# A transformer block on one core: the operands of the MLP's two products as two scaled fp16 pieces instead of two fp32r pieces

## The chip, the core and the metric

The kernel runs on one core of one Trainium2 chip. The core has five engines: TensorE (PE in the profile, with its weight loads as PEld), VectorE (DVE), ScalarE (ACT), GpSimd (POOL) and SyncE (SP), which issues most DMA transfers here. Each engine takes its instructions in order. The metric is the time of one execution on the device in microseconds (us), the median of several.

## What is computed

One block of a transformer for 1024 tokens of width 1024, with float32 in and out:

```python
n = rms_norm(h, norm1_g[layer])
proj = jnp.einsum('bsd,dp->bsp', n, w_in[layer])
...
y = jnp.concatenate([rms_norm(ya, out_norm_a_g[layer]),
                     rms_norm(yb, out_norm_b_g[layer])], axis=-1)
h = h + jnp.einsum('bsm,md->bsd', y, w_out[layer])
n2 = rms_norm(h, norm2_g[layer])
u = jnp.square(jax.nn.relu(jnp.einsum('bsd,df->bsf', n2, w_ff1[layer])))
h = h + jnp.einsum('bsf,fd->bsd', u, w_ff2[layer])
...
return rms_norm(h, final_norm_g)
```

`ya` and `yb` are two groups of attention heads (a sliding window with learned sinks, and chunks with a relative bias). The change is in the last three lines before the final norm: the norm `n2`, the product with `w_ff1` (1024x4096), the squared ReLU, and the product with `w_ff2` (4096x1024).

## The kernel before

The input projection, the attention and the output projection come first (to about 427 us); the change leaves them alone, but its first instructions stand among the last of the output projection. There, for each block `tb` of 128 tokens, PE makes `op_B` (group B's part), and `rows2(tb)` does the rest: DVE multiplies the sum by `rB` (the norm of group B, a short chain of 128x8 operations from `ss_B`) and adds the residual row `h`, ACT takes the sum of squares, `rstd` makes the factor `r` (`u_n2` on ACT, four small operations on DVE), ACT copies the row for its way to DRAM (`hB`), and DVE writes the normed row `n2`. PE transposes pairs of such rows into banks `tp` (two of them), ACT copies them to the tiles `F00` to `F21`, and `operand` splits them, and sums of them, into the operands `X`.

Each product of the MLP is blocked, and each block of two by two parts is multiplied with seven products instead of eight (the numbers 1 to 7; `second_operands` forms the sums and differences of the parts of the weights, `T` for w1 and `Z` for w2). Product 1 goes over eight blocks `n` of 512 hidden columns (`order1`), product 2 over four groups `g` of two such blocks (`order2`). Every one of the 7 x 8 products in each half is 24 matmuls of 128x128 by 128x512: float32 is written as the sum of two pieces, and three of the four products of pieces are taken:

```python
        matmul(ps, a[0], b[0], start=start, stop=False, skip_group_check=shared)
        matmul(ps, a[0], b[1], start=False, stop=False, skip_group_check=shared)
        matmul(ps, a[1], b[0], start=False, stop=stop, skip_group_check=shared)
```

`split` makes the pieces: the high one by a copy on ACT (which rounds), the low one by a subtraction on POOL or DVE. Their type is fp32r before. Operands are named `X` (input of product 1), `W` (its weights, from `T` or a tile `w1`), `U` (the hidden values, read back from DRAM as `u`) and `V` (the weights of product 2, from `Z` or a tile `w2`). The epilogue of product 1 (in `product1`) adds on DVE, takes ReLU and square on ACT, forms the sums for the seven products of the next step in tiles `k` and `v`, and stores them to DRAM (`put`). In product 2, `add_up` adds each finished bank to an accumulator `C` on DVE; `final` makes the last norm.

Operands are prepared two or three products ahead (`AHEAD1`, `AHEAD2`), the loads of `u` three (`LOAD2`). The program's text gives the tile scheduler the order; it may move instructions within what the dependences and the buffers allow, so the order on each engine is shown below where it matters. A buffer pool with a count (`bufs`) makes its next user wait until the oldest tile is free: three pairs of PSUM banks `ab`, two banks `tp`.

## Time and profile before

| | us |
|---|---|
| median of 3 runs (1049.77 to 1051.04) | 1049.78 |
| the profiled execution | 1049.81 |
| its span | 1048.0 |
| first matmul of product 1 / of product 2 | 427.2 / 736.5 |

The profile shows one execution. A row of a group gives source line, engine, operation, output <- inputs, shapes, the count, then the time busy in total and the mean duration in ns. A row of the timeline begins with the start and the duration in us. What an engine waited for is given in brackets or, in the view of waits, as the total, the number and the longest wait.

### The profile page before, as it was taken

How to read it: one execution, taken by the hardware profiler on the slowest of the kernel's cores; microseconds unless marked ns; L12 is line 12 of the kernel's file. 1: busy time of each engine (PE TensorE's matmuls, PEld its weight loads, DVE VectorE, ACT ScalarE, POOL GpSimd, SP SyncE). 2: the span in 40 equal slices, each digit the busy share in tenths (PEclk: the TensorE clock that was granted, in tenths of full speed). 3: DMA queues.
4: the chain of work that ended last, by engine and by line, in shares of the span. 5: the costliest groups of instructions: out<-in, count | busy, mean ns of one | idle time of the engine just before them, and what ended most of it. 6: DMA issues, size and time to landing. Idle time of an engine off the chain costs nothing.

```text
span 1048.0 us, 13827 instructions
## 1 busy us (share of the span) xinstructions
PE 1022.3 (98%) x4803; PEld 829.6 (79%) x4803; DVE 711.9 (68%) x1063; ACT 581.5 (55%) x969; POOL 426.0 (41%) x327
## 2 busy tenths in 40 slices
PE   9999999999988999999999999999999999999997
PEld 7888887777655778878888888887888888888886
DVE  6576787877676635885644554566878777687667
ACT  8676766767567757574454454455523333333346
POOL 0466665243353555015445444545114023124025
PEclk9999999999999999999999999999999999999999
DMA  9944537999999982325524533436996445533004
GB/s 356 252 133 124 141 75 180 199 220 214 225 242 231 221 269 93 119 81 181 181 101 161 181 130 133 178 117 220 375 397 254 147 136 179 170 133 101 1 1 161
DMA packets 141574, 183.77 MB, mean 175 GB/s; under 512 B 78016, under 2 KB 95424, under 8 KB 141504
## 3 DMA queue, kind: packets, MB, share of 16 engines
q1 hardware_dynamic: 141360, 182.63, 58.3%
q8 instruction: 38, 0.62, 0.2%
q14 instruction: 32, 0.26, 0.1%
q10 hardware_dynamic: 144, 0.26, 0.1%
HBM read 103.17 MB, written 42.99 MB: 139 GB/s over the span
## 4 chain that ended last, share of the span: by engine, by line
PE 58%; issue 4%; DVE 1%; ACT 1%; DMA 1%; POOL 0%; ACTq 0%; DVEq 0%; POOLq 0%
PE f L167 24%; PE f_a L167 16%; PE f_c L167 8%; PE op_B L167 4%; PE f_b L167 4%; DMA G_B<-H_B 1%; POOL W L173 0%; PE tp L170 0%; DVE V L173 0%; DVE Z L1245 0%; DVE T L1245 0%; PE end L167 0%; PE op_A L167 0%; DVE k L1316 0%; PE ss_B L167 0%
## 5 line engine op out<-in xcount | busy, mean ns | idle before, releaser
L167 PE MATMUL f<-X,W 128*128 128x512 f32 x1344 | 306.4, 390 | 1.8 <-POOL W L173 1.1
L167 PEld LDWEIGHTS f<-X,W 128*128 128x128 f32 x1344 | 251.9, 188 | 55.1 <-POOL W L173 1.5
L167 PE MATMUL f_a<-V,U 128*128 128x512 f32 x756 | 173.5, 389 | 0.0
L173 POOL TENSOR_TENSOR U<-u,U 128x1024 fp32r<-128x1024 f32 x32 | 80.1, 2502 | 224.9 <-PE f_c L167 135.0
L167 PEld LDWEIGHTS f_a<-V,U 128*128 128x128 f32 x756 | 141.9, 188 | 29.7 <-DVE C L1560 0.3
L173 POOL TENSOR_TENSOR W<-T,W 128x1024 fp32r<-128x1024 f32 x29 | 76.4, 2636 | 103.3 <-ACT W L1267 91.2
L167 PE MATMUL f_c<-V,U 128*128 128x512 f32 x384 | 88.4, 389 | 0.0
L173 POOL TENSOR_TENSOR W<-w,W 128x1024 fp32r<-128x1024 f32 x23 | 59.5, 2587 | 68.8 <-ACT W L1267 62.9
L1267 ACT ACTIVATE V<-Z 128x1024 fp32r<-128x1024 f32 x32 | 33.9, 1060 | 90.3 <-PE f_a L167 44.6
L167 PEld LDWEIGHTS f_c<-V,U 128*128 128x128 f32 x384 | 72.1, 188 | 15.0
L1316 DVE TENSOR_TENSOR k<-f,k 128x1024 f32<-128x1024 f32 x24 | 29.4, 1223 | 79.7 <-PE f L167 42.5
L1267 ACT ACTIVATE W<-T 128x1024 fp32r<-128x1024 f32 x32 | 33.9, 1059 | 66.2 <-PE f L167 26.4
L1267 ACT ACTIVATE V<-w 128x1024 fp32r<-128x1024 f32 x24 | 25.5, 1061 | 81.2 <-issue 34.2
L173 DVE TENSOR_TENSOR V<-w,V 128x1024 fp32r<-128x1024 f32 x24 | 48.9, 2039 | 28.0 <-ACT V L1267 24.6
L167 PE MATMUL op_A<-w_o,y 128*128 128x512 f32 x192 | 57.6, 427 | 8.6 <-DVE ts_vB L427 4.7
L1267 ACT ACTIVATE U<-u 128x1024 fp32r<-128x1024 f32 x56 | 58.5, 1044 | 7.2 <-DMA u<-ud 7.2
L614 ACT ACTIVATE P_B<-P_B,nm_B 128x640 f32<-128x640 f32 (+2 forms) x64 | 44.2, 690 | 29.9 <-DVE nm_B L611 15.0
L859 DVE SCALAR_TENSOR_TENSOR H_B<-P_B,rc_B,H_B 128x640 f16<-128x640 f32 (+2 forms) x64 | 51.7, 836 | 10.4 <-ACT H_B L854 10.0
L167 PE MATMUL ip_qB<-nT,w_qB 128*128 128x512 f32 x192 | 53.8, 406 | 1.1 <-DVE t_kB L401 1.0
L167 PE MATMUL ip_kB<-nT,w_kB 128*128 128x512 f32 x192 | 53.7, 404 | 0.0
L1267 ACT ACTIVATE W<-w 128x1024 fp32r<-128x1024 f32 x24 | 25.3, 1060 | 48.3 <-PE f L167 42.1
L167 PE MATMUL ip_vB<-nT,w_vB 128*128 128x512 f32 x192 | 51.2, 400 | 0.0
(242 smaller groups left out, 1950.2 us busy)
## 6 DMA issues: line engine op xcount, KB each, us to landing
w<-in_w_ff_dram SPq DMA_DIRECT2D x64, 512.0 KB, 4.6
u<-ud SPq DMA_DIRECT2D x56, 512.0 KB, 4.5
ud<-k SPq DMA_DIRECT2D x48, 512.0 KB, 2.9
KkB<-t_kB SPq DMA_DIRECT2D x32, 256.0 KB, 5.1
xr<-in_x_dram SPq DMA_DIRECT2D x8, 512.0 KB, 8.8
st_o<-in_w_out_dram SPq DMA_DIRECT2D x8, 512.0 KB, 5.0
h<-in_x_dram SPq DMA_DIRECT2D x8, 512.0 KB, 4.7
hB<-h SPq DMA_DIRECT2D x8, 512.0 KB, 2.6
```

The source lines that it names most:

```text
L167: pe(nc.tensor.matmul(*args, **kw))
L173: return engine.tensor_tensor(lo, full, f(hi), ALU.subtract)
L614: nc.scalar.activation(pr, pr, AF.Exp, bias=nm, scale=-1.0, accum_out=sm)
L859: nc.vector.scalar_tensor_tensor(lo, q, rc, hi, ALU.mult, ALU.subtract)
L1267: nc.scalar.activation(w[0], full, AF.Copy)
L1316: dve.tensor_tensor(v, ps, v, ALU.add)
```

## The change

All pieces become fp16, and both pieces of an operand lie in one tile. To keep them in fp16's range, each operand is first multiplied by a power of two that is made from the maximum of the data: of g2b, the gain of the norm, for the input (`scale_of_x`, into `xup`, which goes into the norm's factor), of each block of w1 (`see1`, `scale1`: four tiles reduced on DVE, then scaled in place on ACT), of u in each group (maxima taken in the epilogue of product 1, `scale_of_u`), and of w2 in each group (`see2`, `scale2`: eight tiles reduced, the factor `up2` goes into the split). A maximum over all partitions is made by `send`: a column of 128x1 goes to DRAM by SP's queue and is read back to all partitions (128x128, the tile `all`), and `bits` reduces that row on DVE (`topall`). The inverse factors leave with the ReLU (`down1`) and with the sums of product 2 (`down2`). The split on DVE with a factor is a scalar_tensor_tensor; where POOL splits U, ACT scales the tile in place first. The loads of w1 and w2 come earlier: all of `load1(1)` at row block 4, and w2 for a whole group ahead of it, one tile for each product.

```diff
--- before.py
+++ after.py
@@
+PAD = 88
+X_UP, W_UP, U_UP = 7, 12, 11
@@
-    small.tile([P, 8], F32, tag="pad", bufs=1, name="pad")
+    small.tile([P, PAD], F32, tag="pad", bufs=1, name="pad")
@@
+    def bits_of(top, name, least=-90):
+
+        nc.vector.tensor_scalar(top, top, 2.0**least, None, ALU.max)
+        e = small.tile([P, 1], F32, tag="e", bufs=2, name=f"e_{name}")
+        nc.vector.tensor_scalar(e.bitcast(I32), top.bitcast(I32), 0xFF << 23, None, ALU.bitwise_and)
+        return e
+
+    def power(dst, e, by, plus):
+
+        nc.vector.tensor_scalar(dst.bitcast(I32), e.bitcast(I32), float(by), float(plus << 23), ALU.mult, ALU.add)
+        return dst
...
+    class Top:
...
+        def see(self, src):
+            nc.vector.tensor_reduce(self.column(), flat(src), mybir.AxisListType.X, ALU.max, apply_absolute_value=True)
+
+        def send(self):
...
+            nc.vector.tensor_reduce(top, self.cols[:, : self.n], mybir.AxisListType.X, ALU.max)
+            nc.sync.dma_start(tops[self.slot].rearrange("a p -> p a"), top)
+            self.all = small.tile([P, P], F32, tag="all", bufs=1, name=f"all_{self.name}")
+            nc.sync.dma_start(self.all, tops[self.slot][0].partition_broadcast(P))
+
+        def bits(self, least=-90):
+            top = small.tile([P, 1], F32, tag="topall", bufs=3, name=f"topall_{self.name}")
+            nc.vector.tensor_reduce(top, self.all, mybir.AxisListType.X, ALU.max)
+            return bits_of(top, self.name, least)
@@
         r = rstd(ss, D, 1, f"n2_{tb}")
+        nc.vector.tensor_tensor(r, r, xup, ALU.mult)
@@
-            X[p] = [[page([P, 2, HALF], f"X{p}{hl}{i}") for i in range(2)] for hl in range(2)]
-        hi, lo = (X[p][hl][g][:, :, part(n)] for hl in range(2))
+            X[p] = [page16([P, 2, 2, HALF], f"X{p}{i}") for i in range(2)]
+        hi, lo = (X[p][g][:, hl, :, part(n)] for hl in range(2))
         nc.scalar.activation(hi, src, AF.Copy)
-        split_l(engine, lo, src, hi)
+        engine.tensor_tensor(lo, src, hi, ALU.subtract)
@@
+    def see1(n, blocks=((0, 0), (0, 1), (1, 0), (1, 1))):
...
+        for b in blocks:
+            top1[n].see(w1s[(n, *b)])
+        if top1[n].count == 4:
+            top1[n].send()
+
+    def scale1(n):
+        e = top1.pop(n).bits()
+        up1 = power(scale_tile("up1", str(n), 2), e, -1.0, 254 + W_UP)
+        down1[n] = power(scale_tile("down1", str(n), 3), e, 1.0, -W_UP)
+        nc.vector.tensor_tensor(down1[n], down1[n], xdown, ALU.mult)
+        for b in ((0, 0), (0, 1), (1, 1), (1, 0)):
+            w = w1s[(n, *b)]
+            nc.scalar.activation(w, w, AF.Copy, scale=up1)
@@
-    def split(full, name, engine, alloc):
-        w = [alloc(f"{name}{hl}", hl) for hl in range(2)]
-        nc.scalar.activation(w[0], full, AF.Copy)
-        split_l(engine, w[1], full, w[0])
+    def split(full, name, engine, alloc, up=None):
+        w = alloc(name)
+        w = [w[:, hl] for hl in range(2)]
+        if up is not None and engine is pool:
+            nc.scalar.activation(full, full, AF.Copy, scale=up)
+            up = None
+        nc.scalar.activation(w[0], full, AF.Copy, scale=1.0 if up is None else up)
+        if up is None:
+            engine.tensor_tensor(w[1], full, w[0], ALU.subtract)
+        else:
+            engine.scalar_tensor_tensor(w[1], full, up, w[0], ALU.mult, ALU.subtract)
         return w
@@
         if p == 4:
-            nc.scalar.activation(v, ps, AF.Relu)
+            nc.scalar.activation(v, ps, AF.Relu, scale=down1[n])
+            dve.tensor_reduce(top, ps, mybir.AxisListType.X, ALU.max)
         else:
-            dve.tensor_tensor(v, ps, v, ALU.add)
-            nc.scalar.activation(v, v, AF.Relu)
+            dve.tensor_tensor_reduce(v, ps, v, 1.0, 0.0, ALU.add, ALU.max, top)
+            nc.scalar.activation(v, v, AF.Relu, scale=down1[n])
@@
+    scale_of_x()
     rows2(0)
     rows2(1)
     load1(0)
@@
         rows2(tb)
+        if tb in (2, 3):
+            see1(0, ((tb - 2, 0), (tb - 2, 1)))
+        if tb == 4:
+            scale1(0)
         if tb in (4, 5):
             prepare1(0, tb - 3, tb - 4)
-        if tb == 5:
-            load1(1, ((0, 0),))
+        if tb == 4:
+            load1(1)
+        if tb in (6, 7):
+            see1(1, ((tb - 6, 0), (tb - 6, 1)))
+    scale1(1)
     prepare1(1, 1, 2)
-    load1(1, ((0, 1), (1, 0), (1, 1)))
@@
+    def see2(g, tiles):
...
+    def scale_of_u(g):
...
+    def scale2(g):
+        e = top2.pop(g).bits(-30)
+        up2[g] = power(scale_tile("up2", str(g), 2), e, -1.0, 254 + W_UP)
+        down2[g] = power(scale_tile("down2", str(g), 2), e, 1.0, -W_UP)
+        nc.vector.tensor_tensor(down2[g], down2[g], udown[g], ALU.mult)
@@
-        ops2[n, p] = split(a, f"U{n}_{p}", pool if p in (1, 2, 3, 4) else dve, high), split(b, f"V{n}_{p}", dve, third)
+        ops2[n, p] = (
+            split(a, f"U{n}_{p}", pool if p in (1, 2, 3, 4) else dve, high, uup[g]), split(b, f"V{n}_{p}", dve, high, up2[g])
+        )
@@
-        if p == 3 and n > 0:
+        if p == (1 if n > 1 else 5) and n:
             load1(n + 1)
@@
+        if 0 < n < NQ - 1:
+            if p == 6:
+                see1(n + 1)
+            if p == 7:
+                scale1(n + 1)
+        if p == 5 and n and n % GQ == 0:
+            scale_of_u(n // GQ - 1)
+        if (n, p) in ((NQ - 2, 4), (NQ - 1, 1)):
+            for tile2 in blocks2(0)[(p == 1) * 4 :][:4]:
+                load2w(*tile2)
         if n == NQ - 1:
+            if p in (5, 6):
+                see2(0, blocks2(0)[(p == 6) * 4 :][:4])
@@
-        return fp.tile(shape, dt, tag="pg3", bufs=10, name=name)
+        return fp.tile(shape, dt, tag="pg3", bufs=13, name=name)
@@
-        nc.vector.tensor_tensor(flat(c), flat(ps), flat(c), ALU.add)
+        nc.vector.scalar_tensor_tensor(flat(c), flat(ps), down2[g], flat(c), ALU.mult, ALU.add)
@@
     for at, (g, p, n) in enumerate(order2[:-GQ]):
         fetch2(at + LOAD2)
+        step = at % (7 * GQ)
+        if g + 1 < NQ // GQ:
+            if step in range(1, 9):
+                load2w(*blocks2(g + 1)[step - 1])
+            if step in range(3, 11):
+                see2(g + 1, blocks2(g + 1)[step - 3 :][:1])
+            if step == 12:
+                scale2(g + 1)
...
+        if (g, step) == (0, 4):
+            scale_of_u(NQ // GQ - 1)
         prepare2(at + AHEAD2)
```

Where the instructions stand now is shown at three places.

DVE at the end of the output projection of group B. `w_gB` to `rB` is the chain of group B's norm, `op_B_0` and `op_B_1` are the sums of the first two row blocks (`h0`, `h1` their residual rows), `tops_w1_n<-w1_n_..` the reduction of one tile of w1's block n. Before:

```order
L185 TENSOR_SCALAR w_gB_4323<-ss_B_4313 128x8
L186 RECIPROCAL q_gB_4324<-u_gB_4322 128x8
L190 TENSOR_TENSOR w_gB_4323<-w_gB_4323,q_gB_4324 128x8
L191 TENSOR_TENSOR w_gB_4323<-w_gB_4323,u_gB_4322 128x8
L192 RECIPROCAL rB_4252<-w_gB_4323 128x8
L1150 SCALAR_TENSOR_TENSOR op_B_0_4275<-op_B_0_4275,rB_4252,h0_3587 128x1024
L1150 SCALAR_TENSOR_TENSOR op_B_1_4294<-op_B_1_4294,rB_4252,h1_3704 128x1024
```

After (the reductions of the four tiles of w1_0 and that of g2b stand right ahead of this piece):

```order
L1163 TENSOR_REDUCE top_w1_0_4539<-tops_w1_0_4452 128x1
L1140 TENSOR_SCALAR xup__4291<-e_x_4364 128x1
L1140 TENSOR_SCALAR xdown__4292<-e_x_4364 128x1
L1158 TENSOR_REDUCE tops_w1_1_4730<-w1_1_00_4603 128x1
L187 TENSOR_SCALAR w_gB_4341<-ss_B_4331 128x8
L188 RECIPROCAL q_gB_4342<-u_gB_4340 128x8
L192 TENSOR_TENSOR w_gB_4341<-w_gB_4341,q_gB_4342 128x8
L193 TENSOR_TENSOR w_gB_4341<-w_gB_4341,u_gB_4340 128x8
L194 RECIPROCAL rB_4268<-w_gB_4341 128x8
L1207 SCALAR_TENSOR_TENSOR op_B_0_4293<-op_B_0_4293,rB_4268,h0_3603 128x1024
L1170 TENSOR_REDUCE topall_w1_0_4586<-all_w1_0_4542 128x1
L1207 SCALAR_TENSOR_TENSOR op_B_1_4312<-op_B_1_4312,rB_4268,h1_3720 128x1024
```

Ahead of the chain there are now four reductions of 128x1024 for w1_0, one for w1_1 and those for g2b, and the row that needs w1_0's maximum back from DRAM (`topall_w1_0`) stands between the sums of row blocks 0 and 1.

ACT a little later, from the square of row block 0 on (`u_n2_..` is the root in the norm's factor of a row block, `F00` the copy of the first transposed bank). Before:

```order
L1152 ACTIVATE h0_3587,ss2_0_4344<-op_B_0_4275 128x1024
L182 ACTIVATE u_n2_0_4347<-ss2_0_4344,eps4_78 128x1
L1154 ACTIVATE h0_3587<-op_B_0_4275 128x1024
L1152 ACTIVATE h1_3704,ss2_1_4360<-op_B_1_4294 128x1024
L182 ACTIVATE u_n2_1_4363<-ss2_1_4360,eps4_78 128x1
L1154 ACTIVATE h1_3704<-op_B_1_4294 128x1024
L1196 ACTIVATE F00_4431<-tp_00_00_4432 128x2x256
```

After:

```order
L1209 ACTIVATE h0_3603,ss2_0_4369<-op_B_0_4293 128x1024
L184 ACTIVATE u_n2_0_4372<-ss2_0_4369,eps4_78 128x1
L1212 ACTIVATE h0_3603<-op_B_0_4293 128x1024
L1209 ACTIVATE h1_3720,ss2_1_4386<-op_B_1_4312 128x1024
L1315 ACTIVATE w1_0_00_4402<-w1_0_00_4402,up1_0_4591 128x1024
L1315 ACTIVATE w1_0_01_4404<-w1_0_01_4404,up1_0_4591 128x1024
L1315 ACTIVATE w1_0_11_4408<-w1_0_11_4408,up1_0_4591 128x1024
L1315 ACTIVATE w1_0_10_4406<-w1_0_10_4406,up1_0_4591 128x1024
L184 ACTIVATE u_n2_1_4389<-ss2_1_4386,eps4_78 128x1
L1212 ACTIVATE h1_3720<-op_B_1_4312 128x1024
```

Four scalings of w1_0 stand between the square of row block 1 and its root; `u_n2_1` comes four rows of 128x1024 later. The same four for w1_1 stand further on between `h6`'s square and `u_n2_6`, ahead of `h7`'s square and `F20`, the first bank of the last four row blocks.

DVE near the end of group 0 of product 2 (`C` are accumulators, `f2_0_a` PE's banks, `Z` and `V` weights of the next group, `up2_1` their factor). Before:

```order
L1482 TENSOR_TENSOR C110_6876<-f2_0_a_0_6834,C110_6876 128x1024
L1245 TENSOR_TENSOR Z3_6_7483<-w2_3_11_7443,Z3_5_7405 128x1024
L1245 TENSOR_TENSOR Z2_7_7591<-w2_2_11_7403,w2_2_01_7325 128x1024
L1482 TENSOR_TENSOR C111_6878<-f2_0_a_1_6835,C111_6878 128x1024
L173 TENSOR_TENSOR V0_41_7218<-Z0_4_7211,V0_40_7217 128x1024
L1245 TENSOR_TENSOR Z3_7_7629<-w2_3_11_7443,w2_3_01_7363 128x1024
L173 TENSOR_TENSOR V1_41_7258<-Z1_4_7251,V1_40_7257 128x1024
L1482 TENSOR_TENSOR C000_6830<-f2_0_b_0_7221,C000_6830 128x1024
L1482 TENSOR_TENSOR C001_6832<-f2_0_b_1_7222,C001_6832 128x1024
L173 TENSOR_TENSOR V2_11_7296<-w2_2_00_7249,V2_10_7295 128x1024
```

After:

```order
L1158 TENSOR_REDUCE tops_w2_2_7760<-w2_5_00_7834 128x1
L1624 SCALAR_TENSOR_TENSOR C111_7142<-f2_0_a_1_7101,down2_0_6988,C111_7142 128x1024
L1158 TENSOR_REDUCE tops_w2_2_7760<-w2_5_01_7872 128x1
L1170 TENSOR_REDUCE topall_w2_1_7568<-all_w2_1_7492 128x1
L1133 TENSOR_SCALAR topall_w2_1_7568<-topall_w2_1_7568 128x1
L1135 TENSOR_SCALAR e_w2_1_7571<-topall_w2_1_7568 128x1
L1140 TENSOR_SCALAR up2_1_7573<-e_w2_1_7571 128x1
L1140 TENSOR_SCALAR down2_1_7575<-e_w2_1_7571 128x1
L1528 TENSOR_TENSOR down2_1_7575<-down2_1_7575,udown_1_6044 128x1
L1322 TENSOR_TENSOR Z2_5_7646<-w2_2_01_7172,w2_2_00_7130 128x1024
L1158 TENSOR_REDUCE tops_w2_2_7760<-w2_5_11_7909 128x1
L1352 SCALAR_TENSOR_TENSOR V2_1_7582<-w2_2_00_7130,up2_1_7573,V2_1_7582 128x1024
```

Before, DVE's rows here are the sums of finished banks, the differences `Z` and the splits. Now reductions for group 2 (`tops_w2_2`) stand among them, and `V2_1`, the weights of group 1's first product, follows the row that needs group 1's maximum from DRAM (`topall_w2_1`) and the five that make its factors.

95 lines of the change are left out of this document (75 added, 20 removed).

## The prediction

> **What bounds the kernel now.** First the page, then what TensorE (PE) waits for from the output projection of group B (376 us) to the end, then the busy time of each engine stage by stage.
>
> ```profile
> span 1048.0 us, 13827 instructions
> PE 1022.3 (98%) x4803; PEld 829.6 (79%) x4803; DVE 711.9 (68%) x1063; ACT 581.5 (55%) x969; POOL 426.0 (41%) x327
> ...
> PE f L167 <- POOL W L173: 1.1, 1, 1.1
> PE f L167 <- DVE k L1316: 0.5, 1, 0.5
> PE op_B L167 <- ACT o L1049: 0.2, 1, 0.2
> ...
> 503.00:541.00 38.00, 38.00 (x170) 31.47 (x169) 19.62 (x12) 18.52 (x18) 18.08 (x8) 1.00 0.43 152
> 693.00:737.00 44.00, 43.46 (x192) 35.68 (x191) 32.10 (x19) 25.43 (x27) 22.68 (x8) 1.00 0.58 204
> 737.00:813.00 76.00, 76.00 (x337) 62.96 (x336) 61.86 (x47) 28.27 (x29) 20.95 (x8) 1.00 0.91 339
> 813.00:889.00 76.00, 76.00 (x337) 62.93 (x336) 57.72 (x43) 28.01 (x28) 19.28 (x8) 1.00 0.47 153
> ```
>
> PE waits 1.8 us in 672 us. A window's columns are PE, weight loads, DVE, ACT, POOL (each busy us and instructions), the granted clock, DMA share and GB/s. So in the MLP a faster matmul moves the end at once, as long as the next engine follows, and that is DVE: 61.86 of 76 us busy in group 0 of product 2, 19.6 of 38 in product 1. ACT and POOL stay below half. The profiled execution took 1049.8 us, 1.8 outside its span, and equals the median; the sum starts there.
>
> **Matmuls.** Both products are these groups, all 512 columns wide and all fp32r before; a tail of 24 half-wide ones (12 full ones in work) is left out.
>
> ```profile
> L167 PE MATMUL f<-X,W 128*128 128x512 f32 x1344 | 306.4, 390 | 1.8 <-POOL W L173 1.1
> L167 PE MATMUL f_a<-V,U 128*128 128x512 f32 x756 | 173.5, 389 | 0.0
> L167 PE MATMUL f_c<-V,U 128*128 128x512 f32 x384 | 88.4, 389 | 0.0
> L167 PE MATMUL f_b<-V,U 128*128 128x512 f32 x192 | 44.2, 389 | 0.0
> ...
> 375.38 0.66 PE L167 MATMUL av_B<-G_B,VvB 128*128 128x384 f16 x5
> L167 PE MATMUL av_B<-G_B,VvB x8: 219/300/390, 374.1 to 375.8; 128*128 128x512 f16 x2, 128*128 128x384 f16 x2, 128*128 128x256 f16 x2, 128*128 128x128 f16 x2
> ```
>
> An instruction counts in a window when it overlaps it, so the 337 of 737 to 813 share 76 us plus one duration of 0.389: 76.39/337 = 226.7 ns from start to start. For fp16 only the attention has rows. The five at 375.38 are 384, 256, 256, 128 and 128 wide; the last lasts 0.219, so the first four, 1024 columns, take 0.66 - 0.22 = 0.44 us, 220 ns for 512 columns with two starts in it. One start costs 2 to 3 ns if the rest is proportional to the columns, which leaves some 217 and, with the rounding of 0.44, 213 to 220; I take 215. 2676 + 12 matmuls times 11.7 ns is **31.4 us** gained, half in each product (18 at 220 ns, 37 at 213).
>
> The Trainium skill (TensorE: Matmul & The Clock Gate, "Wait — 56ns, not 53.3ns?") gives any warm matmul N/2.4 GHz plus 2.5 ns, 215.7 for 512 columns, and names no type that needs more. By it fp32r would run so already and the gain be nothing; the 226.7 ns here speak against that, the 0.44 us agree for fp16. It is the rival "no faster" below.
>
> **Start of the MLP.** In the rows of the order, DVE now reduces tiles of w1 ahead of rB, and ACT scales four tiles between h1's square and u_n2_1. Before, the same place ran so:
>
> ```profile
> 386.37 0.27 ACT L182 ACTIVATE u_gB<-ss_B,eps 128x8 f32<-128x8 f32 x1 [5.17 <-PE ss_B L167]
> 387.38 0.20 DVE L192 RECIPROCAL rB<-w_gB 128x8 f32<-128x8 f32 x1
> 387.88 2.67 DVE L1150 SCALAR_TENSOR_TENSOR op_B<-op_B,rB,h 128x1024 f32<-128x1024 f32 x2 [0.29 <-PE op_B L167]
> 392.60 0.30 ACT L182 ACTIVATE u_n<-ss,eps 128x1 f32<-128x1 f32 x1
> 393.89 1.28 DVE L1160 SCALAR_TENSOR_TENSOR n<-op_B,r_n,g2b 128x1024 f32<-128x1024 f32 x1 [0.29 <-ACT h L1154]
> 395.87 0.60 PE L170 MATMUL tp<-ident,n 128*128 128x128 f32 x4
> ...
> 382.41 0.37 SPq L123 DMA_DIRECT2D w<-in_w_ff_dram  x1
> DMA to landing us min/median/max: 7.3/7.6/10.1
> ...
> L432 DVE TENSOR_REDUCE top_vB<-ts_vB 128x1 f32<-128x1024 f32 x4 | 4.9, 1218 | 0.1
> L445 ACT ACTIVATE hvB<-ts_vB,up_vB 128x1024 f16<-128x1024 f32 x4 | 4.6, 1138 | 0.2 <-DVE up_vB L435 0.2
> hB<-h SPq DMA_DIRECT2D x8, 512.0 KB, 2.6
> ```
>
> The load of w1_1_00 is the one issued at 382.41; with the shortest landing, 7.3, it is there at 389.7. Its reduction (1.22) and that of w1_0_11 just before stand ahead of the rB chain, with five small ones: rB about 392.4 instead of 387.6, op_B_0's sum 392.7 to 394.0. Then topall_w1_0 waits for a column that goes to DRAM and back: two transfers. No transfer that small has a row; two of the lightest (2.6) are 5.2, the other end is nothing, and I take 5, since the size hardly shows in 2.6 us for 512 KB. Sent near 390, back near 395.2; op_B_1's sum ends about 396.8. ACT: square 1.2, four scalings at 1.14 with a pointer for the scale, 4.5, u_n2_1 starts about 402.4. Before, 2.6 us later (392.60 to 395.17) n2_1 was done, so now about 405.1 with xup's product, and PE's transposition starts there, not at 395.87: **9.2 us** (8.3 if the round trip costs nothing; the reductions and scalings alone make it).
>
> Later, the same with w1_1:
>
> ```profile
> 421.62 1.03 ACT L1152 ACTIVATE h<-op_B 128x1024 f32<-128x1024 f32 x1 [3.36 <-DVE op_B L1150]
> 423.87 0.59 ACT L1205 ACTIVATE F<-tp 128x512 f32<-128x512 f32 x1
> 426.37 1.04 PE L170 MATMUL tp<-ident,n 128*128 128x128 f32 x8
> ...
> 330.87 0.98 PE L167 MATMUL op_A<-w_o,y 128*128 128x512 f32 x3 [2.16 <-ACT o L1049]
> 331.00:334.00 3.00, 3.00 (x12) 1.89 (x13) 2.30 (x5) 3.00 (x7) 1.08 (x1) 0.72 0.86 189
> 334.00:336.00 2.00, 2.00 (x10) 1.48 (x9) 2.00 (x2) 1.03 (x2) 1.88 (x2) 0.57 1.09 230
> ```
>
> After op_B_6's square (421.62 to 422.85) ACT has four scalings 4.5, u_n2_6 0.3, the copy 1.0 and h7's square 1.2 ahead of F20: 429.9, done 430.5. PE's second eight transpositions need its bank, and started at 426.37: **4.2 us**, and nothing covers them, since all products come after. Each wait also costs clock: after 2.16 us of idle PE got 0.72 for 3 us and 0.57 for 2, 0.8 + 0.9 = **1.7 us**, twice. The start costs 16.8 in all; the bounds are 8 (no round trip, w1_1's scalings in a gap, one drop) and 22 (round trips as slow as the 10.1 us above).
>
> **Product 1, then.** Per n of 36.1 us DVE gains four reductions, 4.9, one for u's maximum, 1.2, and some ten small ones at 0.15 to 0.2: 27.5 us, and a wait of 5 for the round trip. It fits; ACT goes from 18.5 to 23. I take 0.5, with 4 as the other end.
>
> **Product 2.** Between 693 and 889 DVE was busy 32.10 + 61.86 + 57.72 = 151.7 us. The rows of the order add there the reductions of w2 for groups 0, 1 and 2 (24 x 1.218 = 29.2), some 42 small ones (7), 40 splits and sums that take a scale (0.06 each, 2.4: n's 1.28 against 1.22) and the end of the last n (1.5): 192 us. The 196 us are now 196 x 215/226.7 = 186. **DVE is 6 us short** where PE was the bound. Below that lies the lead in the ready buffers, which may pay it all; above it lie DVE's waits, since it takes its rows in order: topall_w2_1 stands ahead of V2_1, which group 1's first product needs, and waits for a round trip while DMA is 0.91 busy. DVE idled 14 of the 76 us then. I take **10**, with 0 and 25 as ends. Group 2 and 3 have fewer reductions and catch up. ACT gains eight scalings of U per group, 28 to 37 of 72 us, which is no bound. On SP the loads of w2 move a group ahead, one tile for each product, and the two transfers of a maximum stand between them and the loads of u; the second waits for the first to land, 2.6 us by the light row, while u is asked for three products (15 us) ahead: nothing, as long as that lead holds. The end gains a few 128x1 products: 0.4.
>
> Whether a split with a scale costs 1.28 hangs on these:
>
> ```profile
> L1531 DVE SCALAR_TENSOR_TENSOR fo<-C,rf,gains 128x512 f32<-128x512 f32 x4 | 2.9, 741 | 0.0
> L1216 DVE TENSOR_TENSOR S<-S,F 128x512 f32<-128x512 f32 x4 | 2.7, 682 | 0.0
> L859 DVE SCALAR_TENSOR_TENSOR H_B<-P_B,rc_B,H_B 128x512 f16<-128x512 f32 x8 | 7.2, 896 | 0.0
> ```
>
> 0.06 more at 512 columns; H_B, which reads two tiles of SBUF, has 896, some 0.2 more. At the most 0.4 for 1024 columns would make 16 us of the 40: inside the upper end.
> The Trainium skill (Vector Engine (DVE) Microarchitecture Reference, "7. Points that are easy to get wrong") says that a scalar-tensor-tensor with two SBUF sources that are not bf16 runs at half the rate; the 896 ns for H_B are not twice 682, so the trace does not bear it out.
>
> **Sum.** 1049.8 - 31.4 + 16.8 + 0.5 + 10 + 0.4 = 1046.1.
>
> **Rivals.**
> *All hidden*: the tiles of w1 may land early enough for the rows in front of rB to run before 386.67, and DVE's lead pays for the rest: 1049.8 - 31.4 + 0.4 = 1019. For it: DVE idles a third of the span. Against: the rows in front of rB.
> *Only the start*: DVE's lead covers product 2: 1036.
> *Slower, DVE the bound of group 0 and 1*: its waits cannot be filled, 25 us and more: 1061. It turns the sign once product 2's wait is over 31.4 - 17.7 = 14 us, that is if 8 of the 44 us that DVE idled from 693 to 889 stay, beside the 6. For it: 61.86 of 76 with a saturated DMA; against: most of DVE's idle time there was waiting for PE, which ends when DVE is late.
> *Matmuls no faster*: the first fp16 after an fp32r one starts its successor as late as before, and only runs of up to six are shown. Interval 226.7: 1049.8 + 16.8 + 0.9 = 1067.5, product 2 having the old time again.
> *Scaled splits at half the rate*: 40 x 1.2 more, 1094.
>
> **How the numbers follow.** My forecast 1046 (1039 to 1052) has 0.44; all hidden 0.06; only the start 0.20 (1029 to 1039); slower by DVE 0.20 (1052 to 1068); no faster 0.07; half rate 0.03. Range 1029 to 1064: 0.2 is left out (all hidden, no faster, half rate and the upper edge of the slower case). Within 0.2% (1047.7 to 1051.9, about what a measurement here can tell from no change) lies 0.14 of the forecast's 0.44; faster is the rest of it below, 0.28, with 0.26 of two rivals, 0.54; slower the others and its edge, 0.32.
>
> **What would show it.** In the profile after: windows of 76 us in product 2 that hold 355 matmuls ((76 + 0.38)/0.215) instead of 337; PE op_B or tp waiting for DVE n or op_B near 395 to 405 for 9 us and near 430 for 4; in product 2 PE f_a and f_c waiting for DVE V or U, 10 us in all, DVE over 90% busy between 690 and 800. No wait near 395 would fell the start; waits on ACT or POOL instead of DVE would fell the step on product 2; 337 matmuls in 76 us the gain.

## The result and the profile after

The changed kernel is slower: the median of its four runs is 1144.91 us (1143.59 to 1152.16) against 1049.78 us (1049.72 to 1051.04), a ratio of 1.0917 with a 95% interval of 1.0871 to 1.0964. The profiled execution was the longest of the four, 1152.16 us, so that sums over its trace are some 7 us longer than the median.

The first view is the page of the changed kernel: its span and the busy time of each engine, and the chain that ended last.

```profile
span 1150.1 us, 13982 instructions
...
PE 1025.8 (89%) x4803; PEld 598.2 (52%) x4803; DVE 766.8 (67%) x1299; ACT 656.9 (57%) x1033; POOL 403.9 (35%) x327
...
PE 25%; DMA 22%; DVE 15%; issue 6%; ACT 6%; POOL 1%; SPq 0%; DVEq 0%; ACTq 0%; POOLq 0%
```

No engine is a bound by its work: DVE is busy for 67% of the span, less than the 68% of before. PE now idles 1150.1 - 1025.8 = 124.3 us, where it idled 25.7. PE's busy time did not fall either (it was 1022.3), although a matmul that follows another became faster, as the second window below shows: the granted clock has a mean of 0.948, and was 0.996. And DMA stands in the chain with 22%, next after PE. Two windows show both halves of this: PE, weight loads, DVE, ACT, POOL (busy us and instructions), clock, DMA share, GB/s.

```profile
617.00:655.00 38.00, 30.19 (x127) 12.87 (x125) 18.12 (x26) 17.25 (x17) 15.68 (x7) 0.87 0.43 137
1035.00:1073.00 38.00, 38.00 (x178) 17.25 (x177) 31.29 (x20) 22.66 (x22) 19.92 (x8) 1.00 0.15 52
```

Where PE is fed, late in product 2, 178 matmuls take (38 + 0.379)/178 = 215.6 ns each: the forecast interval was 215. In product 1 the same 38 us hold 127 matmuls, at a clock of 0.87. So the gain is there, and something stops PE. The longest waits of DVE and then those of PE, from 376 us to the end, in the changed kernel, name it: who waited, for whom, us in all, times, the longest.

```profile
DVE topall_w L1170 <- DMA all_w<-top: 73.9, 12, 11.0
DVE topall_u L1170 <- DMA all_u<-top: 41.6, 4, 11.4
DVE topf L1402 <- ACT v L1401: 38.4, 6, 10.3
DVE tops_w L1158 <- DMA w<-in_w_ff_dram: 29.1, 17, 4.2
...
PE f L169 <- DVE topf L1404: 26.9, 5, 7.2
PE f L169 <- ACT k L1394: 18.5, 2, 9.9
PE f_a L169 <- DVE C L1624: 14.3, 8, 6.3
PE tp L172 <- ACT F L1263: 12.9, 2, 12.2
PE op_B L169 <- DVE w_n L187: 10.3, 1, 10.3
```

At each of its 16 reads of a returned maximum DVE stood still, 73.9 + 41.6 = 115.5 us in all. PE's own waits do not name those reads. They name rows that DVE and ACT run later: the epilogue `topf` and the sums `C` on DVE, and the copy `k` on ACT. The timeline of the changed kernel shows how the one turns into the other (start, us, queue or engine, line, operation; in brackets the idle time ahead and what ended it). First the start of the MLP:

```profile
389.25 0.34 SPq L1164 DMA_DIRECT2D top<-top_w  x1
396.31 0.34 SPq L1166 DMA_DIRECT2D all_w<-top  x1
...
400.81 0.29 DVE L1170 TENSOR_REDUCE topall_w<-all_w 128x1 f32<-128x128 f32 x1 [8.12 <-DMA all_w<-top]
401.01 1.28 DVE L1207 SCALAR_TENSOR_TENSOR op_B<-op_B,rB,h 128x1024 f32<-128x1024 f32 x1
...
404.75 2.90 PE L169 MATMUL op_B<-w_o,y 128*128 128x512 f32 x6 [10.32 <-DVE w_n L187]
407.44 0.41 PE L172 MATMUL tp<-ident,n 128*128 128x128 f32 x1
```

The column of 128 words goes out at 389.25. The read back can be asked for only at 396.31, when the store has landed, and has landed at 400.81: 11.6 us. Meanwhile op_B's sum and the norm of row block 0, all of whose inputs are there, stand behind topall_w, and PE waits 10.3 us. Then a place in product 1:

```profile
598.53 0.32 SPq L1164 DMA_DIRECT2D top<-top_w  x1
...
606.10 0.32 SPq L1166 DMA_DIRECT2D all_w<-top  x1
...
599.67 1.23 DVE L1418 TENSOR_TENSOR k<-k,k 128x1024 f32<-128x1024 f32 x1
611.48 0.29 DVE L1170 TENSOR_REDUCE topall_w<-all_w 128x1 f32<-128x128 f32 x1 [10.58 <-DMA all_w<-top]
...
624.28 1.21 DVE L1404 CUSTOM_DVE_ANT_0 k<-f,k 128x1024 f32<-128x1024 f32 x1
...
625.56 14.80 PE L169 MATMUL f<-X,W 128*128 128x512 f16 x55 [7.20 <-DVE topf L1404]
```

Sent at 598.53, back 13 us later; DVE stands 10.6 us of them, is then behind with the sums `T`, reductions and the epilogue (and waits 3 us more, for ACT's scaling and for a load of w1), and PE stands 7.2 us, until 14 us after the read, for a bank that the epilogue has not emptied. The lengths of the transfers themselves are in the DMA view (count, KB each, median us from issue to landing):

```profile
all_w<-top SPq DMA_DIRECT2D x12, 64.0 KB, 4.8
...
top<-top_w SPq DMA_DIRECT2D x12, 0.5 KB, 8.1
top<-top_u SPq DMA_DIRECT2D x4, 0.5 KB, 9.0
```

512 bytes take 8 to 9 us to DRAM in the median, where 512 KB of h took 2.6 in the kernel before. Single round trips, from the store's issue to the landing of the read back, lasted 11.2 to 22.3 us.

### The profile page after: what moved, and what is told of

The parts are those of the page before. It is cut to its first block, busy times and chain, and to the rows that moved or that the text cites. A ratio compares the mean times of both kernels' runs of the same rounds, so it can differ in the third digit from the quotient of the medians.

```text
span 1150.1 us, 13982 instructions
## 1 busy us (share of the span) xinstructions
PE 1025.8 (89%) x4803; PEld 598.2 (52%) x4803; DVE 766.8 (67%) x1299; ACT 656.9 (57%) x1033; POOL 403.9 (35%) x327
## 4 chain that ended last, share of the span: by engine, by line
PE 25%; DMA 22%; DVE 15%; issue 6%; ACT 6%; POOL 1%; SPq 0%; DVEq 0%; ACTq 0%; POOLq 0%
PE f L169 9%; DMA top<-top_w 5%; PE f_a L169 4%; DMA all_w<-top 4%; PE op_A L169 4%; DVE tops_w L1158 3%; DMA top<-top_u 3%; DMA w<-in_w_ff_dram 3%; PE f_c L169 3%; DMA u<-ud 3%; PE f_b L169 2%; DVE V L1352 2%; DVE C L1624 2%; ACT w L1315 2%; DVE Z L1322 1%
## 5 line engine op out<-in xcount | busy, mean ns | idle before, releaser
L169 PE MATMUL f<-X,W 128*128 128x512 f16 x1344 | 308.5, 394 | 47.4 <-DVE topf L1404 26.9
L169 PEld LDWEIGHTS <-W 128*128 128x128 f16 x1344 | 135.3, 101 | 219.6 <-issue 69.3
L169 PEld LDWEIGHTS <-U 128*128 128x128 f16 x1356 | 133.6, 99 | 194.7 <-issue 31.8
L169 PE MATMUL f_a<-V,U 128*128 128x512 f16 x756 | 169.7, 385 | 16.6 <-DVE C L1624 14.3
L1350 POOL TENSOR_TENSOR U<-u,U 128x1024 f16<-128x1024 f32 x32 | 76.2, 2388 | 244.0 <-ACT U L1348 200.9
L1350 POOL TENSOR_TENSOR W<-T,W 128x1024 f16<-128x1024 f32 x29 | 68.5, 2375 | 205.3 <-ACT W L1348 192.1
L169 PE MATMUL f_c<-V,U 128*128 128x512 f16 x384 | 87.6, 390 | 10.7 <-DVE C L1624 5.4
L1158 DVE TENSOR_REDUCE tops_w<-w 128x1 f32<-128x1024 f32 x64 | 75.9, 1212 | 29.2 <-DMA w<-in_w_ff_dram 29.1
L1350 POOL TENSOR_TENSOR W<-w,W 128x1024 f16<-128x1024 f32 x23 | 52.2, 2271 | 46.5 <-ACT W L1348 46.5
L617 ACT ACTIVATE P_B<-P_B,nm_B 128x640 f32<-128x640 f32 (+2 forms) x64 | 44.2, 691 | 29.7 <-DVE nm_B L614 15.3
L169 PE MATMUL op_B<-w_o,y 128*128 128x512 f32 x192 | 50.3, 417 | 10.5 <-DVE w_n L187 10.3
L862 DVE SCALAR_TENSOR_TENSOR H_B<-P_B,rc_B,H_B 128x640 f16<-128x640 f32 (+2 forms) x64 | 51.7, 836 | 10.4 <-ACT H_B L857 10.2
L1170 DVE TENSOR_REDUCE topall_w<-all_w 128x1 f32<-128x128 f32 x12 | 3.4, 286 | 73.9 <-DMA all_w<-top 73.9
```

The lines of the kernel that those rows point to most:

```text
L169: pe(nc.tensor.matmul(*args, **kw))
L617: nc.scalar.activation(pr, pr, AF.Exp, bias=nm, scale=-1.0, accum_out=sm)
L862: nc.vector.scalar_tensor_tensor(lo, q, rc, hi, ALU.mult, ALU.subtract)
L1158: nc.vector.tensor_reduce(self.column(), flat(src), mybir.AxisListType.X, ALU.max, apply_absolute_value=True)
L1350: engine.tensor_tensor(w[1], full, w[0], ALU.subtract)
```

## The experiments

The theory after this reading: (A) the round trip is 12 us and more, not 5, and DVE, which takes its rows in order, stands for it in front of work that PE needs. Rivals: (B) the added DVE work itself (reductions, splits with a scale) is too much; (C) the scalings and splits are late because their factor is late, whether DVE stands or not; (D) fp16 or the other new operations cost something of their own; (E) the trip holds up SP's queue, since its second transfer is issued only when the first has landed, and the loads behind it come late. No run was made for E alone; what the traces say of it stands under unused. The runs compare three stages, each measured by first starts of PE's groups: the start up to the first `f`, product 1 from there to the first `f_a`, and product 2 from there to the last matmul.

| kernel | time, us | first `f` at | product 1 | product 2 |
|---|---|---|---|---|
| before | 1049.8 | 427.2 | 309.3 | 304.8 |
| after | 1144.9 (profiled 1152.2) | 458.5 | 357.1 | 328.0 |
| unused | 1117.9 | 455.2 | 332.4 | 321.6 |
| no_trip | 1050.8 | 436.3 | 308.7 | 297.3 |
| no_maxima | 1040.3 | 440.8 | 295.9 | 295.2 |
| const_start | 1028.7 | 431.4 | 295.8 | 293.8 |
| const_start5 | 1029.2 | 429.1 | 295.8 | 295.6 |
| idle_read | 1058.9 | 453.1 | 304.0 | 293.5 |
| trip_early | 1141.5 | 456.5 | 348.8 | 326.9 |
| pe_turn | 1112.7 | 433.9 | 355.4 | 314.9 |
| pe_turn_later | 1072.8 | 432.3 | 303.1 | 327.7 |
| ahead | 1067.5 | 432.5 | 323.5 | 299.2 |
| sizes | 1059.6 | 442.6 | 307.3 | 301.1 |
| layout | 1063.5 | 436.7 | 309.9 | 308.2 |

Only `after`, `const_start5`, `const_start` and `ahead` have several runs; the others are single runs, taken beside runs of the kernel before at 1047.9 to 1049.4 us. const_start and const_start5 are the same kernel, and their stages differ by up to 2.3 us; differences of two or three us between single runs are not read.

**no_trip** takes out the transfers, and with them the wait for the factors, which are constants; all reductions stay, and the read reduces a tile of zeros, so that it waits for nothing.

```diff
-            nc.sync.dma_start(tops[self.slot].rearrange("a p -> p a"), top)
-            self.all = small.tile([P, P], F32, tag="all", bufs=1, name=f"all_{self.name}")
-            nc.sync.dma_start(self.all, tops[self.slot][0].partition_broadcast(P))
...
-            nc.vector.tensor_reduce(top, self.all, mybir.AxisListType.X, ALU.max)
+            nc.vector.tensor_reduce(top, nought, mybir.AxisListType.X, ALU.max)
```

> The changed kernel without the two transfers of each maximum: the reductions stay, but the row that reduces the returned maximum reads a constant tile in SBUF, and the powers of two come from constants that bound this data. Theory 1 (VectorE, in order, stands still until the maximum is back, 74 + 42 us in the trace, and PE's clock falls in every gap): 1035 to 1060 us, with the start still late by the reductions and scalings, and product 1 near 36 us for each n. Theory 2 (the added work of VectorE is the bound, the waits only show where it is late): 1110 us or more. Theory 3 (the loads of w1 and w2 that now come earlier collide with others): also 1110 or more, with waits on the DMA of w and u.

1050.8 us, inside the first range, although product 1 takes 38.6 us for each n and not 36: 94 us of the time of the changed kernel are the transfers and what waits for them. The DVE work that remains is 785.7 us busy, and still the kernel is as fast as before; so B does not carry the loss. It carries a part of what the kernel could gain: in group 0 of product 2 DVE was full, and that window of no_trip holds 340 matmuls instead of the 354 that PE could do at 215.6 ns.

```profile
745.00:821.00 76.00, 73.62 (x340) 32.91 (x339) 75.02 (x66) 42.99 (x41) 19.35 (x8) 1.00 0.82 300
```

Its start, 9.1 us later than before, is not the start without trips alone. The factor is a constant, so four of ACT's scalings of w1_0 no longer wait for it; they run ahead of `u_gB` in ACT's queue, group B's norm, which began behind `u_gB` at 386.37 before, begins at 393.76, and PE waits for it:

```profile
393.76 0.17 DVE L187 TENSOR_SCALAR w_gB<-ss_B 128x8 f32<-128x8 f32 x1 [1.43 <-ACT u_gB L184]
...
PE op_B L169 <- DVE q_n L188: 8.2, 1, 8.2
```

**no_maxima** takes out the reductions of the tiles of w1 and w2 too (64 of 1.21 us, `see`).

```diff
         def see(self, src):
-            nc.vector.tensor_reduce(self.column(), flat(src), mybir.AxisListType.X, ALU.max, apply_absolute_value=True)
+            self.count += 1
```

> As no_trip, and the reductions of the tiles of w1 and w2 (64 of 1.2 us) left out too: fp16 pieces, scalings and scaled sums stay, the powers of two are constants. Theory 1: 10 to 20 us below no_trip, about 1025, because then only the start and the reductions of group 0 are left; theory 2: the whole of the loss goes here, to about 1025 from 1110; theory 3: still 1110.

1040.3 us, 10.5 less, where 1025 was expected. Product 1 fell by 12.8, so the reductions are not hidden there; product 2 fell by 2.1; the start rose by 4.5, since five of ACT's scalings of w1, with a constant factor, now run ahead of `u_gB`, one more than in no_trip:

```profile
389.53 5.32 ACT L1318 ACTIVATE w<-w,up 128x1024 f32<-128x1024 f32 x5 [8.08 <-DVE down L1140]
...
396.16 0.27 ACT L184 ACTIVATE u_gB<-ss_B,eps 128x8 f32<-128x8 f32 x1
```

**const_start** mends that: it holds ACT's scalings of the first two blocks behind the copies of rows 1 to 3 and 5 to 7. It also takes a constant for the maximum of g2b.

```diff
+    def behind_row(ins, names, tb):
+        dep = mybir.DependencyInfo(mybir.DependencyClass.NoSync, mybir.DependencyReason.DATA)
+        tc.add_manual_dep(ins.ins, names[tb], dep, reason="program order")
...
-            nc.scalar.activation(w, w, AF.Copy, scale=up1)
+            ins = nc.scalar.activation(w, w, AF.Copy, scale=up1)
+            if n < 2:
+                behind_row(ins, row_act, ((1, 2, 2, 3), (5, 6, 6, 7))[n][i])
```

> no_maxima (constants for the powers of two, also for the norm's gain), with the eight scalings of w1's first two blocks held behind the copies of the row blocks on ScalarE. There the start was still 13.6 us late (440.8 against 427.2). If the place of the scalings in ScalarE's queue is what makes the start late, first f at 427 to 431 and 1028 to 1032 us in all; if the start is late for another reason (the longer order of small rows, the loads), first f stays near 440 and the time at 1040.

1028.69 us, 0.9811 (0.9779 to 0.9843) of the kernel before, with the first `f` at 431.4 instead of 440.8. The same kernel again:

> const_start again, for its interval: 1027 to 1030 us against 1048 to 1050, a ratio of 0.979 to 0.983 under every theory.

1029.2 us (1028.19 to 1030.24, five runs), 0.9807 (0.9794 to 0.982). This is the version that beats both kernels. It does not do what the change does: its factors are constants, which must be bounds of the data (|w1| under 1/4, |w2| under 1/8, u ahead of the square under 32) instead of being made from it. Its page and its rows for product 1:

```profile
PE 994.3 (97%) x4803; PEld 588.0 (57%) x4803; DVE 706.4 (69%) x1223; ACT 654.3 (64%) x1033; POOL 408.8 (40%) x328
...
L169 PE MATMUL f<-X,W 128*128 128x512 f16 x1344 | 290.9, 379 | 2.0 <-DVE X L1256 1.3 <-DVE topf L1415 0.7
```

So D is out as the cause of the loss: with fp16, the scaled splits, ACT's 32 scalings of w1 and the sums with a factor in place, products 1 and 2 are 13.5 and 9.2 us shorter than before. And the run splits the loss of the changed kernel: by the two profiled executions PE idles 124.3 us against 1027.0 - 994.3 = 32.7, and is busy 1025.8 against 994.3 with the same 4803 matmuls. Of 123 us, 92 are waits of PE, and 31 are longer busy time, which comes with a mean granted clock of 0.948 against 0.995.

**unused** does everything that the changed kernel does (reductions, transfers, the read of what comes back), but uses constants. It keeps DVE's standing and the transfers and takes away the late factor.

```diff
-            nc.vector.tensor_reduce(top, self.all, mybir.AxisListType.X, ALU.max)
+            unused = small.tile([P, 1], F32, tag="topback", bufs=2, name=f"topback_{self.name}")
+            nc.vector.tensor_reduce(unused, self.all, mybir.AxisListType.X, ALU.max)
+            nc.vector.tensor_reduce(top, nought, mybir.AxisListType.X, ALU.max)
```

> The changed kernel with every reduction, both transfers of each maximum and VectorE's row that reads it, but nothing uses that row's result: the powers of two come from constants, as in no_trip. Between no_trip (1051, product 1 308.7 us, product 2 297.3) and the changed kernel (1145, 357 and 328) only two things differ: VectorE stands until the maximum is back (here too), and the scalings, splits and products wait for the factor (here not). If standing still is most of it, 1120 to 1145 and product 1 above 340; if the late factor is, 1060 to 1080 and product 1 at 312 to 325; idle_read (eight trips without reductions) had 303.8 against 295.6 in product 1 and lost 24 in the start.

1117.9 us, between the two ranges: neither A nor C is all of it. Of the 94 us of the trips, 67 (1117.9 - 1050.8) are there although nothing uses what comes back, and 27 (1144.9 - 1117.9) only when something does. By stages the 67 are 18.9 in the start, 23.7 in product 1 and 24.3 in product 2; the late factor is felt in product 1 above all (24.7 of its stages' 34.4, which are 7 longer than the medians' difference). In the start it may be worth more than the 3.3 of the table, because here, as in no_trip, ACT's scalings run ahead of `u_gB`. The waits of this kernel, with nobody using what is read:

```profile
DVE topback_w L1171 <- DMA all_w<-top: 66.7, 10, 10.9
...
DVE topback_u L1171 <- DMA all_u<-top: 31.7, 4, 11.2
```

The 67 us hold DVE's standing (A) and the loads that come late behind the trip (E): SP's queue stands 83.5 us here, as in the changed kernel (82.1), until a store has landed and the read back can be issued. In product 1 the loads are a small part: DVE waits 3.5 us for tiles of w1 and ACT 5.4 us for u (2.4 and 0.8 in no_trip), while DVE stands 59.6 us for the reads. So there it is mostly the standing. In product 2 the two are not told apart: DVE stands 19.2 us for the reads, but ACT also waits 52.9 us for loads of u, where it is 34.2 in no_trip, and DVE 16.5 us for tiles of w2, where it is 9.6.

**idle_read** comes from the other side: const_start, with eight trips (the two of the start and six in product 1) whose result is read in the same places and not used.

```diff
+            nc.vector.tensor_reduce(top, w1s[(n, 1, 1)][:, 0, :8], mybir.AxisListType.X, ALU.max)
+            nc.sync.dma_start(tops[n].rearrange("a p -> p a"), top)
+            back[n] = small.tile([P, P], F32, tag="all", bufs=1, name=f"all_w1_{n}")
+            nc.sync.dma_start(back[n], tops[n][0].partition_broadcast(P))
...
+        nc.vector.tensor_reduce(unused, back.pop(n), mybir.AxisListType.X, ALU.max)
```

> const_start, in which each block of w1 again sends a column of 128x1 through DRAM and back when its last tile has landed, and VectorE reduces the row that comes back at the place where the changed kernel does, but nothing uses the result (the powers of two are constants). Eight round trips, no reduction of whole tiles. If standing still in VectorE's queue is what costs, 12 us for each of the six blocks in steady state of which the slack of some 16 us per block hides a part: product 1 from 296 to 310 to 360 us, time 1043 to 1090; if it is the late factor (scalings, splits and products wait for it), product 1 stays at 296 to 300 and the time within 6 us of 1029 plus what the start loses.

1058.9 us, 29.7 over const_start5: 24 in the start, 8 in product 1, and product 2 two shorter. Product 1, 304.0, lies between the two ranges expected for it. DVE stood 83.8 us in the eight reads, 61.9 of them in product 1:

```profile
DVE topback_w L1326 <- DMA all_w<-top: 83.8, 8, 12.3
```

In product 1, 62 us of standing cost 8, where in unused 60 us cost 24 (30.9 and 28.7 for w and u there). One difference is what DVE has to do beside: without the reductions it is busy 176 us of that stage, with them 216. The reading that fits is that standing is paid for out of an engine's idle time first, and only what is left over reaches PE; it is not shown alone, since unused also has the trips for u. In the start, 21.9 us of standing cost 24.

**Why the trip is so slow** was looked for twice. **sizes** adds to no_trip a store per maximum that nobody waits for, from a constant tile, of 4, 64 and 512 bytes per partition in turn.

```diff
+            nc.sync.dma_start(wide[self.slot][:, : (1, 16, 128)[self.slot % 3]], nought[:, : (1, 16, 128)[self.slot % 3]])
```

> no_trip with a store to DRAM, which nothing waits for, at each place where a maximum was sent: from a constant tile, 4, 64 or 512 bytes for each of 128 partitions in turn. The transfer of 512 KB in 128 pieces lands after 3.0 us, that of 0.5 KB in 128 pieces after 8.1. If the 4-byte pieces are slow by themselves, 4 bytes land after 7 to 9 us and 512 bytes (64 KB) after 2 to 3, at the same places; if it is the moment (queue behind the loads of w and u), all three land after 7 to 9 us. Time as no_trip, 1051, within 3 us.

Having nothing to wait for, all of these stores ran at 17 to 32 us, before the MLP; so they say nothing of the moment. They landed in 3.7 to 3.9 us in the median whatever their size, but each partition's piece lay in its own 512 bytes of DRAM. The time, 1059.6, was 9 above no_trip; that stays open. **layout** stores the true columns at the true places, again with nobody waiting: half of them as the change does, 128 words side by side, and half with each word 512 bytes from the next.

```diff
+            if self.slot % 2:
+                nc.sync.dma_start(wide[self.slot][:, :1], top)
+            else:
+                nc.sync.dma_start(tops[self.slot].rearrange("a p -> p a"), top)
```

> no_trip, where each maximum's column is also stored to DRAM at its usual moment, and nothing waits for that: for half of them 128 words of 4 bytes side by side as in the changed kernel, for the others each word 512 bytes from the next. If it is words side by side that make the store slow, the first land after 7 to 9 us and the others after 2 to 4; if it is the moment or the size, both after 7 to 9. Time 1048 to 1056.

The view of the tile `top`, and under it that of `wide`, both of layout:

```profile
DMA to landing us min/median/max: 7.2/9.5/10.2
...
DMA to landing us min/median/max: 1.4/2.3/9.7
```

Side by side the 512 bytes take 7.2 us at best; apart, 1.4 to 2.5 in five cases of eight, and 6.9 in one; the two at 9.5 and 9.7 had been queued within 1 us behind a slow store. So the place of the words in DRAM makes the greater part of the slow store, not their number; the moment adds to it. The time, 1063.5, is 12.6 above no_trip although nothing waits for these stores. 10.9 of it lie in product 2, where PE waits 11.3 us before `f_a` for the sums `C` (3.2 in no_trip), and the cause was not found. In the start and in product 1, stores that nobody waits for cost next to nothing (0.4 and 1.2).

**trip_early** was to keep the trip and move it ahead of its use: the maxima of u0 to u2 are read in one place near the end of product 1, from a tile each, and in the program's text w1's loads stand two products and its reductions one product earlier.

```diff
-        if p == (1 if n > 1 else 5) and n:
-            load1(n + 1)
+        if p == 5 and n == 1:
+            load1(2)
+        if p == 2 and n:
+            load1(n + 2)
...
-            if p == 6:
+            if p == (5 if n > 1 else 6):
                 see1(n + 1)
...
-        if p == 5 and n and n % GQ == 0:
-            scale_of_u(n // GQ - 1)
+        if (n, p) == (NQ - 1, 3):
+            for g in range(3):
+                scale_of_u(g)
```

> The changed kernel with all maxima and transfers, but with more room between sending and reading: w1's blocks are loaded and reduced two products earlier, u's maxima of groups 0 to 2 are read only at the end of product 1, with tiles of their own, so that SyncE's queue does not hold w's transfer behind u's. If a round trip costs only where VectorE reads it too early, product 1 falls from 357 us to 300 to 325 and the time to 1090 to 1115; if the transfers disturb whenever they are read, or the tiles for earlier loads are not free, it stays near 1145.

1141.5 us, 3 less than the changed kernel, where 30 to 55 less were expected. The stores moved hardly, from 519.7 to 518.6 and from 555.2 to 554.5 us, because the last tile of a block comes no earlier: for the store at 555 its load is issued at 541.10 instead of 541.98, and it is reduced at 545.09 instead of 545.80, and the column was then made behind the same rows of the epilogue. SP's queue stood 54.1 us for DVE to free the tiles that the loads write to (42.0 in the changed kernel), which is the second branch of what was expected. What u's reads no longer stood (41.6 to 7.8 us) those of w stood instead (73.9 to 95.5).

**pe_turn** leaves DRAM out where it can: DVE spreads the column over 128 columns, PE turns that with the identity into PSUM, DVE reduces the row; only w2 of groups 1 to 3 still goes through DRAM.

```diff
+            nc.vector.tensor_scalar(self.all, ident, 0.0, top, ALU.mult, ALU.add)
+            tp = mps.tile([P, 2, 2 * P], F32, tag="tp", bufs=2, name=f"tp_top_{self.name}")
+            self.row = tp[:, 0, :P]
+            matmul(self.row, self.all, ident, start=True, stop=True)
```

> The maxima stay taken from the data, but in the start, product 1 and for group 0 the column goes to all partitions by TensorE (a 128x128 product of the column, spread over 128, with the identity) instead of through DRAM; the maxima of w2 for groups 1 to 3 still go through DRAM. If the length of the round trip (12 to 22 us) is the cause and not the reading of a maximum as such, product 1 takes 305 to 315 us as in no_trip, and the time is 1065 to 1080, the rest being group 1 to 3's trips; if reading a maximum in order is what costs, product 1 stays above 340.

1112.7, too slow by 32 us and more. The start is mended (433.9, 6.7 later than before). But PE takes its rows in order as well, and the maximum of u comes from an epilogue at the end of a queue; PE stood for it four times, once for 25.6 us between the products, which is why the table has 355.4 for product 1 and the next expectation, which counts to its last matmul, 329:

```profile
PE tp_top_u L169 <- DVE all_u L1169: 43.5, 4, 25.6
```

**pe_turn_later** turns the columns of u0 to u2 at one place near the end of product 1, where they are long done, and reads u3 through DRAM.

```diff
-        if p == 5 and n and n % GQ == 0:
-            scale_of_u(n // GQ - 1)
+        if (n, p) == (NQ - 1, 3):
+            for g in range(3):
+                scale_of_u(g)
+        if (n, p) == (NQ - 1, 4):
+            topu[NQ // GQ - 1].send()
```

> pe_turn, but u's maxima of groups 0 to 2 are turned on TensorE only at the end of product 1, where they have long been made, and that of group 3 goes through DRAM again. In pe_turn TensorE stood 43.5 us at the four rows for u, and 0.5 at all those for w1. If these waits were the whole of what it missed, product 1 goes from 329 to 308 to 314 us and the time to 1060 to 1078; if product 1 is also held by the reductions (the row of the last tile comes late), it stays above 320.

1072.8: the waits are gone from product 1, which takes 303.1 with true maxima of the data, 54 less than in the changed kernel and less than the 308 that was expected. Product 2, which still has the trips for w2 and u3, takes 327.7, as the changed kernel does (328.0). **ahead** removes those too: the tiles of w2 for groups 1 to 3 are loaded a second time and reduced in product 1, and u3's read comes a group later.

```diff
+        if n > 1 and p in (1, 5, 6, 3, 7) and unseen:
+            g, m, i, j = unseen.pop(0)
+            t = page([P, 2, HALF], f"w2ahead_{m}_{i}{j}", F32)
...
-        if (g, step) == (0, 4):
+        if (g, step) == (1, 4):
             scale_of_u(NQ // GQ - 1)
```

> pe_turn_later without any round trip that something waits for in product 2: the 24 tiles of w2 of groups 1 to 3 are also loaded once during product 1 (five for each block from the third on) and reduced there, their maxima turned on TensorE before product 2; only u's maximum of group 3 goes through DRAM, read a whole group later. All powers of two still come from the data. If product 2 of pe_turn_later (327.7 us against 295.8 with constants) loses to the trips and to reductions that stand in VectorE's queue waiting for loads, product 2 takes 295 to 300 us and the time is 1038 to 1050, product 1 having 303 to 312; if it loses to the scaled splits and sums, product 2 stays above 315 and the time at 1065 to 1080.

1067.46 us (1065.02 to 1070.65, four runs), 1.0186 (1.0155 to 1.0216) of the kernel before. Product 2 is at 299.2, as expected. The run takes two things out of product 2 at once, the trips and the reductions, for whose tiles DVE waited 54.2 us in pe_turn_later; no_trip, which keeps the reductions in place, has 297.3, and so points to the trips. Product 1 went to 323.5, beyond what was expected: the 24 loads and reductions more are not free there. So with maxima of the data nothing that was tried here is faster than before.

## Why the prediction was wrong, step by step

**The step that failed** is the price and the place of the round trip: "two of the lightest (2.6) are 5.2, the other end is nothing, and I take 5, since the size hardly shows in 2.6 us for 512 KB". The row it used moves 512 KB in long pieces; the trip moves 128 words of 4 bytes that lie side by side, then reads them into 128 partitions, and lasts 11.2 to 22.3 us. The longest round trip in any range of the prediction, 10.1 us in the upper end of the start, is shorter than that. The view of transfers before had rows nearer in size, 128 pieces of 32 bytes each:

```profile
psink<-in_sinks_a_dram SPq DMA_DIRECT2D x1, 4.0 KB, 9.2
ogc<-in_og_dram SPq DMA_DIRECT2D x1, 4.0 KB, 8.7
```

They are loads, issued near 22 us in the run, but two transfers at that price are some 18 us and not 5. The second half of the mistake stands in product 1: "27.5 us, and a wait of 5 for the round trip. It fits". The sum was right: in no_trip DVE is busy 221.6 us of product 1, 27.7 for each n. But summing busy time into a period of 36 us takes for granted that DVE may fill its idle time with other rows. It takes its rows in order: what fits by the sum stood, 76.5 us in ten reads in product 1 of the changed kernel (42.6 for w, 33.9 for u), and at the place shown came out on PE 14 us later. Product 2's reasoning named that mechanism ("DVE's waits, since it takes its rows in order"), with the wrong price; product 1's did not use it.

**By terms of the sum.** *Matmuls, -31.4.* The interval was right (215.6 against 215). In const_start5 the two products gain 13.5 + 9.2 = 22.7 of it; 1.6 of the rest are the 0.6 ns of the interval, and most of what is left are short waits (PE idles 7.0 us of the two products there, 1.8 before).

*Start, +16.8.* Measured +31.3. The places were right: PE waited for op_B behind topall_w near 395 to 405, and a second time at w1_1's read, which the prediction had charged with its scalings alone (4.2): DVE stood 8.8 us there too, up to 446.33. The transposition that began at 422.76 begins at 439.75, 17.0 later (9.2 + 1.7 forecast); the second place makes it 31.3 (4.2 + 1.7 more forecast). With the maxima turned on PE instead of sent through DRAM the start costs 5.1 to 6.7 (pe_turn, pe_turn_later, ahead), below the 8 that the prediction gave as its lower bound; with constants, no reductions and ACT's order mended, 1.9 and 4.2. That no_trip's 9.1 is near 8 is chance, since its delay is that of `u_gB`.

*Product 1, +0.5.* Measured: 357.1, where 309.3 - 15.7 + 0.5 = 294.1 was expected. The pieces: 295.8 with constants, so that the rest of the step holds; +12.9 for the reductions (no_trip), which were to be hidden, and which alone pass the other end of 4 (5.8 of it is one wait of PE for ACT's scaling of w1); +23.7 for standing; +24.7 for late factors, in profiles that include the 7 us above the median.

*Product 2, +10.* Measured 328.0, where 299.1 was expected. DVE was full in group 0, as forecast, once nothing stopped it (75.02 of 76 us in no_trip), but PE idled only 2.4 us of that window. Without trips the stage takes 297.3, which is 8.2 above the 289.1 of faster matmuls alone and looks like the 10; but without reductions, too, it takes 295.2, so the reductions, the greater part of DVE's added work, are worth some 2 us and not most of the 10. The agreement is luck. What came on top is the trips: 24.3 of standing and late loads, 6.4 of late factor.

*Clock.* The prediction charged 1.7 us for each of two waits. It was the right kind of price, asked too seldom: PE is busy 31 us longer than in const_start5, at a lower granted clock.

*Prices of operations* held: the sum with a factor 1.273 us (1.28 forecast), a split of V with a factor 1.28 in the median, a reduction 1.21 (1.22), a scaling on ACT 1.14. Half-rate splits and unchanged matmuls fall as rivals.

**The rivals.** "Slower" had the right sign and place (DVE's waits for round trips in product 2), but at 1061 and only in product 2, where the trips were priced by the same light row. The turning point it named, 8 us of DVE's idle time that cannot be filled, was passed: DVE stood 14.4 + 7.8 = 22.2 us for trips in product 2.

**What stays open**: how the 24.3 us of product 2 divide between DVE's standing and loads that come late behind the trip; the 9 and 12.6 us of sizes and layout, kernels in which nothing waits for the added stores; why the store of neighbouring words is slow; and how the 27 us of the late factor divide between ACT's scalings and the splits.

## What to carry to other kernels

A maximum over partitions that went through DRAM was a wait of 11 to 22 us here, and any row that waits for it on an in-order engine holds up all that is queued behind: look for what is behind the row, and add it even where the engine's busy time seems to leave room. For a transfer that no row shows, take the bound from pieces of the nearest size and layout, not from the lightest median. And before a number is made from the data inside a loop, time the kernel with a constant in its place: here such runs told that the arithmetic made the kernel 2% faster, and that finding the scale made it 11% slower than that.

## What was not expected of the hardware

- 128 words of 4 bytes from 128 partitions, stored side by side in DRAM, landed after 7.2 to 10.2 us in layout (6.9 to 14.2 in the changed kernel); with 512 bytes between them after 1.4 to 2.5 us in five cases of eight. The read back of 64 KB took 4.8 us in the median.
- 92 us more of PE's waits came with 31 us more of busy time for the same 4803 matmuls, at a mean granted clock of 0.948 against 0.995.
- In product 1, 62 us of standing on DVE went with 8 us of lost time in one kernel, and 60 us with 24 in another that gave DVE 40 us more to do.
